# Packed dt weights, two-phase loading of SSD outputs and joined y products in a hybrid encoder layer

## The chip, the cores and the metric

The kernel runs on one core of a Trainium2 chip. The metric is the time of one execution in device microseconds (us). The programs have been run several times; the profile is one execution, taken by the hardware profiler. Its engines are PE (TensorE, matrix products, with PEld for its weight loads), DVE (VectorE), ACT (ScalarE), POOL (GpSimd) and SP (SyncE, which here issues every DMA).

## The reference, cut to what matters

One encoder layer over two requests of 256 tokens each (`x_prompt`, `x_sample`), model width 1024: a half-step FFN, one input projection `u @ w_in` that feeds three branches (neighbourhood attention, a bidirectional SSD, attention to a memory), a gated merge, and a second half-step FFN. The change touches the SSD branch:

```python
dt_f, dt_b = split_sizes(dt_raw, (SSD_HEADS, SSD_HEADS))          # 32 + 32 columns of u @ w_in
dt_f = softplus(dt_f + dt_bias_f);  a_f = -exp(a_log_f)           # the same for b
y_fwd = ssd_chunked(xs, dt_f, a_f, bm, cm)                        # 32 heads of 64, 8 groups, chunks of 128 tokens
y_bwd = flip(ssd_chunked(flip(xs), flip(dt_b), a_b, flip(bm), flip(cm)))
y_ssd = (y_fwd + y_bwd + ssd_d * xs) * silu(z)
o_ssd = grouped_rms_norm(y_ssd, ssd_norm, SSD_GROUPS)             # 8 groups of 256 channels
merged = g_na * (o_na @ w_br_na) + g_ssd * (o_ssd @ w_br_ssd) + g_mem * (o_mem @ w_br_mem)
```

## The kernel before

Both requests are worked on together: activations lie transposed, channels on the 128 partitions and 512 tokens (2 x 256) in a row. Weights are streamed once, in chunks of 128 x 1024 f32 (512 KB, tile `wr`, one DMA on SP's queue at L290) into a ring of 9 buffers (`RING`). `ahead()` splits each chunk into a high part `wh` (ACT, L322) and a low part `wl` (DVE, L236), and every product is made of three: high by high, high by low, low by high. A unit of the plan is 24 matmuls with 512 columns (L545 to L547 for `m` tiles, L1094 for the SSD branch's output projection), accumulated in one PSUM bank.

`PLAN` lists the units by hand. The side work of a stage (attention, SSD, norms) is a set of generators in a queue (`later`); `step()` moves the active ones on by one `yield` for each unit. The Tile scheduler then sets the order of each engine's instructions from that program order. Each engine and each DMA queue works through its own list in order.

The places that the change touches:

- `warm()` (L423 to L430). 16 matmuls on a zeroed tile `af` stand ahead of the first real product. POOL writes the zeroes (L425), then ACT makes a copy within the same tile so as to load its function table, then come the matmuls `wm` (L429; the profile shows two records for each).
- `do_dt` (L1131) and `t_dt` (L1138 on). The 64 dt columns of `w_in` are a unit of 24 matmuls with 64 output rows. `t_dt` then works softplus out on 64 x 512 tiles, transposes dt and a * dt with 8 transposes (`dtT`, L1166 and L1167) and copies them to `tokd`, tokens on partitions. Bias and a_log come from two columns of `params`.
- `t_ssd` (L1235 on), one generator for each of 8 groups. A group has two channel tiles i = 0, 1 of 128 channels. After the products CB (L1255), ACT and DVE make the decay tiles `e` for 8 cases (i, request b, head half hp). For each i and b, a run of 4 matmuls `y` (L1305) multiplies them: two output halves of 64 rows (hp) by two chunks (st), 8 records in the profile. Both runs of an i write one bank `y`, at steps n = 3, 5, 7 and 9 of the generator. After n = 5 and n = 9 DVE scales and gates the result; `rows_to_cols` (`sum`, L506), `spread` (`dg`, L514) and `spread_mm` (`R`, L523) make the group norm. Groups 0 to 5 write their result to DRAM (`scr_o`), and their norm factors to `scr_n`.
- `t_os(g)` (L1340) brings the results back. For groups 0 to 5 it loads the norm factors (`rw`, L1343), then for each i the result `or` (L1349), scales it at once (`scale_o`, on DVE) and splits it into `osh` (ACT) and `osl` (DVE). Groups 0 to 3 are handled while the eight SSD gates run (the last stage of L545 to L547 units before L1094), groups 4 to 7 after that. ACT turns each gate's bank into `tg` (L251).

Of the kernel before, what the change touches and what calls it, by code (L numbers as in the profile page):

```python
# [16 lines left out]
KD = 8  # L17
# [153 lines left out]
PCOLS = {}  # L171
_n = 0
for _name, _w in (("ffn1", 8), ("mix", 8), ("mem", 8), ("ffn2", 8), ("cw", 160), ("cb", 32), ("qn", 1), ("kn", 1),
                  ("mqn", 2), ("mkn", 2), ("sn", 16), ("dd", 16), ("dtb", 1), ("al", 1)):
    PCOLS[_name] = _n
    _n += _w
NPAR = _n
# [7 lines left out]
class Layer:  # L185
# [126 lines left out]
    def ahead(self, ci):  # L312

        for i in range(self.n_split, min(ci + 3, len(ITEMS))):
            it = ITEMS[i]
            self.fetch(i + self.depth)
            self.sums(i + 1)
            n = it.nk * it.m
            t = self.live[it.src]
            hi = self.pw.tile([128, 1024], F32R, tag="hi", name=self.name("wh"))  # L320
# [56 lines left out]
    def setup(self):  # L377
        nc = self.nc
        self.consts = self.pc.tile([128, NCONST], F32, name="consts")
        self.params = self.pc.tile([128, NPAR], F32, name="params")  # L380
        dma = nc.sync.dma_start
        self.x, self.depth = [], 0
        self.xs_start("ffn1")
        self.warm()
        dma(out=self.params[:, :32], in_=self.a["params"][:, :32])
        for c in range(4):
            for k in (2 * c, 2 * c + 1):
                self.x.append(self.g(p="x"))
# [15 lines left out]
        self.namask = c(8)[:, :64].rearrange("p (n k) -> p n k", n=2)  # L404
        self.lots = self.pc.tile([128, 4, 64], F32, name="lots")
# [723 lines left out]


    def do_dt(self, key, cis):  # L1131
        ps = self.unit(cis, self.u, m=64)

        def evac():
            self.later("dt", self.t_dt(ps))
        return evac

    def t_dt(self, ps):  # L1138
        V, S, T = self.V, self.S, self.T
        r = slice(0, 64)  # L1140
        v, m, e, z, w = (self.g(p="dt") for _ in range(5))
        self.act(v[r], ps[r], AF.Identity, bias=self.par("dtb", 0, r))
        self.ts(m[r], v[r], 0.0, ALU.max)
        self.stt(e[r], v[r], -1.0, v[r], ALU.mult, ALU.min)
        self.act(e[r], e[r], AF.Exp)
        yield
        self.ts(w[r], e[r], 2.0, ALU.add)
        V.reciprocal(w[r], w[r])
        self.tt(z[r], e[r], w[r], ALU.mult)
        yield  # L1150
        self.tt(w[r], z[r], z[r], ALU.mult)
        self.ts(e[r], w[r], 1.0 / 15, ALU.mult)
        for k in (13, 11, 9, 7, 5, 3):
            self.stt(e[r], e[r], 1.0 / k, w[r], ALU.add, ALU.mult)
            if k == 9:
                yield
        self.stt(e[r], e[r], 1.0, z[r], ALU.add, ALU.mult)
        self.stt(v[r], e[r], 2.0, m[r], ALU.mult, ALU.add)
        ea = self.small(2, "ea")
        self.act(ea[r, 0:1], self.par("al", 0, r), AF.Exp)  # L1160
        self.ts(w[r], v[r], ea[r, 0:1], ALU.mult, -1.0, ALU.mult)
# [6 lines left out]
        tk = self.pc.tile([128, 4, 128], F32, name="tokd")  # L1168
        V.tensor_copy(tk.rearrange("p t c -> p (t c)"), ps)
        self.tok = tk  # L1170
        yield
        rs = self.g(p="rs").rearrange("p (b l) -> p b l", b=2)
        for b in range(2):
# [58 lines left out]
    def t_ssd(self, g):  # L1232
# [62 lines left out]
        for n in range(10):  # L1295
            if n < 6:
                rw[n + 2] = self.rows(g, *heads[n + 2])
            if n >= 3 and n % 2:
                i, b, _ = heads[n - 3]
                w = [ws.pop(n - 3), ws.pop(n - 2)]  # L1300
                if b == 0:
                    yb = self.bank("y")
                for st in range(2):
                    for hp in range(2):
                        T.matmul(yb[64 * hp:64 * hp + 64, b * 256:(b + 1) * 256],  # L1305
                                 xt[i][:, (2 * b + st) * 128 + 64 * hp:(2 * b + st) * 128 + 64 * hp + 64],
                                 w[hp][0][:, 2 * st:2 * st + 2, :], start=st == 0, stop=st == 1)
# [12 lines left out]
            yield  # L1320
# [17 lines left out]
        self.stt(v, v, self.half[:, 2 * g + i:2 * g + i + 1], r, ALU.mult, ALU.mult)  # L1338

    def t_os(self, g):  # L1340
        if g < KEEP:
            r, sn = self.g(p="rw"), self.scr_n
            self.nc.sync.dma_start(out=r, in_=bass.AP(sn.tensor, sn.offset + g * 512, [[0, 128], [1, 512]]))  # L1343
        for i in range(2):
            k = 2 * g + i
            t = self.oraw.pop(k, None)
            if t is None:
                t = self.g(p="or")
                self.nc.sync.dma_start(out=t, in_=self.scr_o[k])  # L1349
                self.scale_o(g, i, t, r)  # L1350
            self.os[k] = self.split_tile(t, "os")
        return
        yield


def layer_kernel(tc, aps):
# [7 lines left out]
def layout(inp):  # L1364
# [31 lines left out]
    put("dtb", np.concatenate([f("dt_bias_f")[0], f("dt_bias_b")[0]])[:, None])  # L1396
    put("al", np.concatenate([f("a_log_f")[0], f("a_log_b")[0]])[:, None])

    i = np.arange(128)
    c = np.zeros((128, NCONST), np.float32)  # L1400
# [2 lines left out]
    for k, t in enumerate(tri):  # L1403
# [17 lines left out]
    return {"w": w, "xT": chan("x_prompt", "x_sample"), "memT": chan("mem_prompt", "mem_sample"), "params": p,  # L1421
            "consts": c, "strip": np.ascontiguousarray(strip.reshape(8, 128, 512))}


# [19 lines left out]
```

## Time and profile before

| | |
|---|---|
| time, median of 3 runs | 1757.79 us (1756.99 to 1758.3) |
| the profiled execution | 1756.64 us |
| its span, first to last instruction | 1754.9 us |
| PE busy | 1737.2 us (99%) |
| DVE busy | 1234.6 us (70%) |
| ACT busy | 848.0 us (48%) |
| DMA | 209.69 MB, mean 119 GB/s |

Busy times say how much of the span an engine had an instruction in work. The list of waits says for each engine and line how long it stood idle before such an instruction and what released it, in total, how often, and the longest. The chain of waits is followed back from the last instruction: at each step to what released it. Starts in the chain are moved to the end of what went before, so they can differ by some tenths of a us from the timeline, whose matmul records overlap.

### The profile page before, as it was taken

How to read it: one execution, taken by the hardware profiler on the slowest of the kernel's cores; microseconds unless marked ns; L12 is line 12 of the kernel's file. 1: busy time of each engine (PE TensorE's matmuls, PEld its weight loads, DVE VectorE, ACT ScalarE, POOL GpSimd, SP SyncE). 2: the span in 40 equal slices, each digit the busy share in tenths (PEclk: the TensorE clock that was granted, in tenths of full speed). 3: DMA queues.
4: the chain of work that ended last, by engine and by line, in shares of the span. 5: the costliest groups of instructions: out<-in, count | busy, mean ns of one | idle time of the engine just before them, and what ended most of it. 6: DMA issues, size and time to landing. Idle time of an engine off the chain costs nothing.

```text
span 1754.9 us, 22611 instructions
## 1 busy us (share of the span) xinstructions
PE 1737.2 (99%) x8568; PEld 1419.9 (81%) x8568; DVE 1234.6 (70%) x2056; ACT 848.0 (48%) x1515; POOL 0.7 (0%) x5
## 2 busy tenths in 40 slices
PE   9999999999999999999999999999899999999999
PEld 7888888988788888788877777777688878888887
DVE  7676776876544467835778888888753697776775
ACT  6443443543224336533666766766532464444442
POOL 0000000000000000000000000000000000000000
PEclk9999999999999999999999999999999999999999
DMA  6144233442323232333344545446433234244331
GB/s 258 60 143 144 97 107 134 155 156 89 96 77 104 88 103 85 102 109 97 120 127 127 132 139 136 123 138 175 162 126 121 84 109 138 79 153 127 99 115 48
DMA packets 79708, 209.69 MB, mean 119 GB/s; under 512 B 11120, under 2 KB 19696, under 8 KB 79600
## 3 DMA queue, kind: packets, MB, share of 16 engines
q1 hardware_dynamic: 79600, 208.26, 37.6%
q8 instruction: 67, 1.10, 0.3%
q14 instruction: 41, 0.34, 0.1%
HBM read 198.64 MB, written 9.58 MB: 119 GB/s over the span
## 4 chain that ended last, share of the span: by engine, by line
PE 96%; DVE 2%; DMA 1%; ACT 1%; issue 0%; SPq 0%; DVEq 0%; ACTq 0%
PE ac L567 20%; PE m L545 10%; PE m L546 10%; PE m L547 10%; PE q L589 5%; PE q L591 5%; PE q L590 5%; PE m L1094 5%; PE d L546 5%; PE d L547 5%; PE d L545 5%; PE y L1305 2%; PE hT L692 1%; PE CB L1255 1%; PE q L609 1%; PE q L611 1%
## 5 line engine op out<-in xcount | busy, mean ns | idle before, releaser
L322 ACT CAST wh<-wr 128x1024 fp32r<-128x1024 f32 (+1 forms) x357 | 371.2, 1040 | 686.5 <-PE ac L567 167.1
L236 DVE TENSOR_TENSOR wl<-wr,wh 128x1024 fp32r<-128x1024 f32 (+1 forms) x357 | 431.5, 1209 | 264.4 <-ACT wh L322 259.4
L545 PE MATMUL m<-uh,wh 128*128 128x512 f32 (+1 forms) x584 | 234.9, 402 | 6.7 <-ACT tg L251 6.7
L567 PE MATMUL ac<-wh,sh 128*128 128x512 f32 (+1 forms) x616 | 229.4, 373 | 0.5 <-ACT wh L322 0.5
L546 PE MATMUL m<-ul,wh 128*128 128x512 f32 (+1 forms) x584 | 229.6, 393 | 0.0
L567 PE MATMUL ac<-wl,sh 128*128 128x512 f32 (+1 forms) x616 | 228.1, 370 | 0.7 <-DVE wl L236 0.7
L547 PE MATMUL m<-uh,wl 128*128 128x512 f32 (+1 forms) x584 | 228.5, 391 | 0.0
L567 PE MATMUL ac<-wh,sl 128*128 128x512 f32 (+1 forms) x616 | 228.0, 370 | 0.0
L545 PEld LDWEIGHTS m<-uh,wh 128*128 128x128 f32 (+1 forms) x584 | 109.6, 188 | 38.3 <-ACT tg L251 6.9
L546 PE MATMUL d<-hl,wh 128*128 128x512 f32 x352 | 137.2, 390 | 0.7 <-DVE hl L236 0.7
L545 PE MATMUL d<-hh,wh 128*128 128x512 f32 x352 | 137.4, 390 | 0.5 <-ACT hh L258 0.5
L547 PE MATMUL d<-hh,wl 128*128 128x512 f32 x352 | 137.0, 389 | 0.0
L567 PEld LDWEIGHTS ac<-wl,sh 128*128 128x128 f32 x616 | 116.1, 188 | 20.6 <-DVE wl L236 1.3
L567 PEld LDWEIGHTS ac<-wh,sh 128*128 128x128 f32 x616 | 116.0, 188 | 20.6 <-ACT wh L322 1.3
L567 PEld LDWEIGHTS ac<-wh,sl 128*128 128x128 f32 x616 | 116.0, 188 | 19.7
L547 PEld LDWEIGHTS m<-uh,wl 128*128 128x128 f32 (+1 forms) x584 | 109.6, 188 | 24.6 <-issue 0.4
L546 PEld LDWEIGHTS m<-ul,wh 128*128 128x128 f32 (+1 forms) x584 | 109.7, 188 | 23.6 <-issue 1.5
L247 DVE SCALAR_TENSOR_TENSOR x<-d,x 128x512 f32<-128x512 f32 x96 | 66.2, 690 | 76.5 <-PE d L547 76.0
L589 PE MATMUL q<-wh,uh 128*128 128x512 f32 x256 | 102.9, 402 | 0.0
L236 DVE TENSOR_TENSOR wr<-wr,wr 128x1024 f32<-128x1024 f32 x80 | 97.6, 1221 | 6.3 <-DMA wr<-in_w 5.3
L591 PE MATMUL q<-wl,uh 128*128 128x512 f32 x256 | 99.9, 390 | 0.0
L590 PE MATMUL q<-wh,ul 128*128 128x512 f32 x256 | 99.9, 390 | 0.0
(253 smaller groups left out, 2857.6 us busy)
## 6 DMA issues: line engine op xcount, KB each, us to landing
wr<-in_w SPq DMA_DIRECT2D x308, 512.0 KB
rw<-scr_r SPq DMA_DIRECT2D x64, 256.0 KB
nv<-scr_v SPq DMA_DIRECT2D x64, 64.0 KB
scr_o<-cv SPq DMA_DIRECT2D x12, 256.0 KB
or<-scr_o SPq DMA_DIRECT2D x12, 256.0 KB
wr<-in_w SPq DMA_DIRECT2D x9, 256.0 KB
x<-in_xT SPq DMA_DIRECT2D x8, 256.0 KB
mr<-in_memT SPq DMA_DIRECT2D x8, 256.0 KB
```

The lines of the kernel that those rows point to most:

```text
L236: self.V.tensor_tensor(out=out, in0=a, in1=b, op=op)
L247: self.V.scalar_tensor_tensor(out=out, in0=a, scalar=s, in1=b, op0=op0, op1=op1)
L322: self.S.copy(hi[:, :n], t[:, :n])
L545: self.T.matmul(ps[:m], wh[:, kk, :], xh, start=i == 0, stop=False)
L546: self.T.matmul(ps[:m], wh[:, kk, :], xl, start=False, stop=False)
L547: self.T.matmul(ps[:m], wl[:, kk, :], xh, start=False, stop=i == n - 1)
L567: go = lambda l, r, **f: self.T.matmul(ps, l, r, skip_group_check=True, **f)
L589: self.T.matmul(self.qb[t], xh, wh[:, kk, :], start=k == 0, stop=False)
L590: self.T.matmul(self.qb[t], xl, wh[:, kk, :], start=False, stop=False)
L591: self.T.matmul(self.qb[t], xh, wl[:, kk, :], start=False, stop=k == KD - 1)
L1094: go = lambda l, r, **f: self.T.matmul(ps, l, r, skip_group_check=True, **f)
L1305: T.matmul(yb[64 * hp:64 * hp + 64, b * 256:(b + 1) * 256], xt[i][:, (2 * b + st) * 128 + 64 * hp:(2 * b + st) * 128 + 64 * hp + 64], w[hp ...
```

## The change

There are four edits.

1. **dt.** High and low part of the 64 dt columns lie side by side in one tile of 128 columns. One matmul with the high part of `u` makes high by high and low by high in 128 output rows, a second with the low part of `u` adds to the first 64: 16 matmuls in place of 24. `t_dt` copies the bank, transposes first (4 transposes of 128 x 128) and works softplus out on 128 x 256 tiles; bias and a_log come as a row `dtrow`, broadcast by a new DMA.
2. **y.** The two runs of an i (one for each request) become one run of 8 matmuls, sixteen records, at n = 5 and n = 9.
3. **t_os.** Both `or` loads of a group are issued with the load of the norm factors; after two `yield`s come the scaling and the split.
4. **warm.** ACT's copy works on a small tile `wm` of its own.

```diff
@@ ahead
+            if it.m == 64:
+                both = self.pw.tile([128, 1024], F32R, tag="hi", name=self.name("wh"))
+                v = both.rearrange("p (k m) -> p k m", k=it.nk)
...
+                self.S.copy(v[:, :, :64], raw)
+                self.tt(v[:, :, 64:], raw, v[:, :, :64].bitcast(F32), ALU.subtract)
...
@@ constants
+        self.dtrow = self.pc.tile([128, 128], F32, name="dtrow")
+        rows = self.a["dtrow"]
+        dma(out=self.dtrow, in_=bass.AP(rows.tensor, rows.offset, [[0, 128], [1, 128]]))
@@ warm
-        self.act(z[:, :1], z[:, 1:2], AF.Copy)
+        y = self.small(2, "wm")
+        self.G.memset(y, 0.0)
+        self.act(y[:, :1], y[:, 1:], AF.Copy)
@@ do_dt
-        ps = self.unit(cis, self.u, m=64)
+        ps = self.bank()
...
+        for k in range(KD):
+            xh, xl = self.u[k]
+            self.T.matmul(ps, w[:, k, :], xh, start=k == 0, stop=False, skip_group_check=True)
+            self.T.matmul(ps[:64], w[:, k, :64], xl, start=False, stop=k == KD - 1, skip_group_check=True)
@@ t_dt
+        raw = self.g(p="dt")
+        S.copy(raw, ps)
+        yield
+        ps = self.bank("dtT")
+        for t in range(4):
+            c = slice(t * 128, (t + 1) * 128)
+            T.transpose(ps[:, c], raw[:, c], self.ident)
...
-        for t in range(4):
-            s = slice(t * 128, (t + 1) * 128)
-            T.transpose(ps[:, t * 128:t * 128 + 64], v[r, s], self.ident[r, 0:64])
-            T.transpose(ps[:, t * 128 + 64:(t + 1) * 128], w[r, s], self.ident[r, 0:64])
...
@@ t_ssd
-            if n >= 3 and n % 2:
-                i, b, _ = heads[n - 3]
-                w = [ws.pop(n - 3), ws.pop(n - 2)]
-                if b == 0:
-                    yb = self.bank("y")
-                for st in range(2):
-                    for hp in range(2):
...
+            if n in (5, 9):
+                i = heads[n - 3][0]
+                yb = self.bank("y")
+                for b in range(2):
+                    w = [ws.pop(n - 5 + 2 * b), ws.pop(n - 4 + 2 * b)]
+                    for st in range(2):
+                        for hp in range(2):
...
@@ t_os
+        ks = (2 * g, 2 * g + 1)
         if g < KEEP:
             r, sn = self.g(p="rw"), self.scr_n
             self.nc.sync.dma_start(out=r, in_=bass.AP(sn.tensor, sn.offset + g * 512, [[0, 128], [1, 512]]))
-        for i in range(2):
-            k = 2 * g + i
-            t = self.oraw.pop(k, None)
-            if t is None:
-                t = self.g(p="or")
-                self.nc.sync.dma_start(out=t, in_=self.scr_o[k])
-                self.scale_o(g, i, t, r)
-            self.os[k] = self.split_tile(t, "os")
-        return
-        yield
+            for k in ks:
+                self.oraw[k] = self.g(p="or")
+                self.nc.sync.dma_start(out=self.oraw[k], in_=self.scr_o[k])
+            yield
+            yield
+            for i in range(2):
+                self.scale_o(g, i, self.oraw[ks[i]], r)
+        for k in ks:
+            self.os[k] = self.split_tile(self.oraw.pop(k), "os")
```

On PE, in a middle group of the SSD (`y` is the bank, `e` the decay tiles, `xt` the transposed channels; `m` and `uh`, `ul`, `wh`, `wl` belong to the units between), the runs of one i stand like this before:

```order
L547 MATMUL m1728_9332<-uh654_3388,wl1709_9203 128x512
L1305 MATMUL y1735_9381<-e1705_9192,xt1683_9075 64x256
L1305 MATMUL y1735_9381<-e1714_9254,xt1683_9075 64x256
L1305 MATMUL y1735_9381<-e1705_9192,xt1683_9075 64x256
L1305 MATMUL y1735_9381<-e1714_9254,xt1683_9075 64x256
L545 MATMUL m1737_9398<-uh608_3206,wh1717_9264 128x512
...
L547 MATMUL m1745_9446<-onh1277_6592,wl1731_9336 128x512
L1305 MATMUL y1735_9381<-e1727_9325,xt1683_9075 64x256
L1305 MATMUL y1735_9381<-e1736_9391,xt1683_9075 64x256
L1305 MATMUL y1735_9381<-e1727_9325,xt1683_9075 64x256
L1305 MATMUL y1735_9381<-e1736_9391,xt1683_9075 64x256
L545 MATMUL m1754_9508<-uh608_3206,wh1739_9401 128x512
```

and in the changed kernel like this:

```order
L563 MATMUL m1744_9433<-onh1277_6584,wl1731_9328 128x512
L1330 MATMUL y1751_9475<-e1704_9179,xt1683_9067 64x256
L1330 MATMUL y1751_9475<-e1714_9246,xt1683_9067 64x256
L1330 MATMUL y1751_9475<-e1704_9179,xt1683_9067 64x256
L1330 MATMUL y1751_9475<-e1714_9246,xt1683_9067 64x256
L1330 MATMUL y1751_9475<-e1727_9317,xt1683_9067 64x256
L1330 MATMUL y1751_9475<-e1735_9378,xt1683_9067 64x256
L1330 MATMUL y1751_9475<-e1727_9317,xt1683_9067 64x256
L1330 MATMUL y1751_9475<-e1735_9378,xt1683_9067 64x256
L561 MATMUL m1754_9500<-uh609_3211,wh1738_9388 128x512
```

The first run has moved down by 48 unit matmuls and stands right ahead of the second.

On SP, in the stretch of the SSD gates (`wr` is a weight chunk, `or` an SSD result, `rw<-scr_n` the norm factors of a group), the last loads before the output projection stand like this before:

```order
L290 DMA wr2025_11036<-in_w 128x1024
L1349 DMA or1993_10874<-scr_o_204 128x512
L290 DMA wr2036_11101<-in_w 128x1024
L1349 DMA or1996_10881<-scr_o_204 128x512
L290 DMA wr2041_11134<-in_w 128x1024
L1349 DMA or2003_10912<-scr_o_204 128x512
L1343 DMA rw2054_11230<-scr_n_203 128x512
L1343 DMA rw2065_11277<-scr_n_203 128x512
L290 DMA wr2047_11169<-in_w 128x1024
L1349 DMA or2006_10919<-scr_o_204 128x512
```

and in the changed kernel like this:

```order
L1369 DMA rw1987_10849<-scr_n_208 128x512
L1372 DMA or1988_10851<-scr_o_209 128x512
L1372 DMA or1989_10853<-scr_o_209 128x512
L1254 DMA rw1990_10855<-scr_r_207 128x512
L1369 DMA rw1998_10892<-scr_n_208 128x512
L1372 DMA or1999_10894<-scr_o_209 128x512
L1372 DMA or2000_10896<-scr_o_209 128x512
L290 DMA wr2025_11028<-in_w 128x1024
L290 DMA wr2036_11093<-in_w 128x1024
L290 DMA wr2041_11126<-in_w 128x1024
L290 DMA wr2047_11161<-in_w 128x1024
```

In the first list the last four `or` of the gates alternate with weight chunks, and the last one, `or2006`, stands behind `wr2047`; in the second they stand ahead of `wr2025`. The new `dtrow` load stands behind the `consts` load at the start.

## Rows read from the trace of the kernel before

**Rows 1.** The page: busy time, share of the span and instructions of each engine.
```profile
PE 1737.2 (99%) x8568; PEld 1419.9 (81%) x8568; DVE 1234.6 (70%) x2056; ACT 848.0 (48%) x1515; POOL 0.7 (0%) x5
```
**Rows 2.** Waits of PE: us in total, times, longest.
```profile
PE m L545 <- ACT tg L251: 6.7, 1, 6.7
```
**Rows 3.** Chain of waits at the last SSD gate: start us, us, what.
```profile
1261.53 0.33 SPq L290
1261.92 3.83 DMA or<-scr_o
1265.77 0.76 DVE or L247
1266.56 0.62 ACT osh L258
...
1267.72 0.79 PE m L545
...
1274.82 0.23 PE m L547
```
**Rows 4.** Windows of that wait: length; PE, PEld, DVE, ACT, POOL busy; PEclk, DMA.
```profile
1261.00:1267.70 6.70, 0.00 (x0) 0.00 (x0) 4.33 (x7) 1.76 (x4) 0.00 (x0) 0.75 0.51 158
1267.70:1271.30 3.60, 3.58 (x9) 2.85 (x10) 0.20 (x1) 1.92 (x4) 0.00 (x0) 0.51 0.00 0
1271.30:1275.00 3.70, 3.70 (x18) 3.08 (x17) 0.00 (x0) 0.14 (x1) 0.00 (x0) 1.00 0.00 0
```
**Rows 5.** Waits of SP's queue.
```profile
SPq L290 <- DVE wl L236: 1265.8, 263, 17.5
```
**Rows 6.** Stretches of the SSD gates' end and of a middle SSD group.
```profile
1230.00:1256.00 26.00, 26.00 (x121) 17.79 (x119) 22.41 (x43) 16.78 (x36) 0.00 (x0) 1.00 0.52 170
945.00:997.00 52.00, 52.00 (x249) 40.74 (x248) 44.43 (x93) 35.08 (x74) 0.00 (x0) 1.00 0.50 131
```
**Rows 7.** Chain of waits: a y run, the first and the eleventh matmul behind.
```profile
868.59 1.01 PE y L1305 x8
869.60 0.43 PE m L545
...
872.13 0.23 PE m L546
```
**Rows 8.** Chain of waits: a run of y with 10 records.
```profile
1230.57 1.44 PE y L1305 x10
```
**Rows 9.** Chain of waits: CB alone, and CB right behind a y run.
```profile
845.09 1.73 PE CB L1255 x8
...
894.83 1.92 PE CB L1255 x8
```
**Rows 10.** Timeline of PE: first dt matmul, and the first one behind them.
```profile
455.53 0.40 PE L545 MATMUL m<-uh,wh 128*64 128x512 f32 x1
...
461.05 0.39 PE L589 MATMUL q<-wh,uh 128*128 128x512 f32 x1
```
**Rows 11.** Chain of waits: dt's transposes, the matmul behind, four transposes of 128 x 128.
```profile
493.85 0.20 PE dtT L1166
...
494.49 0.43 PE q L589
...
531.04 0.44 PE amT L868 x4
```
**Rows 12.** Timeline of DVE: the last step of softplus in `t_dt`.
```profile
478.40 0.48 DVE L243 TENSOR_SCALAR dt<-dt,ea 64x512 f32<-64x512 f32 x1
```
**Rows 13.** Timeline of the start: the zeroes on POOL, the warm-up on PE.
```profile
0.73 0.52 POOL L425 MEMSET af<- 128x512 f32 x1 [0.29 <-POOLq L1428]
...
2.28 10.11 PE L429 MATMUL wm<-af 128*128 128x256 f32 x32 [2.28 <-ACT af L251]
```
**Rows 14.** Stretches of the warm-up.
```profile
2.28:8.20 5.92, 5.92 (x14) 4.71 (x15) 2.33 (x5) 3.42 (x7) 0.00 (x0) 1.00 0.95 321
8.20:12.00 3.80, 3.80 (x18) 3.35 (x18) 3.44 (x7) 3.67 (x7) 0.00 (x0) 1.00 1.03 403
```

More of the change, by code (lines that the diff above doesn't have):

```diff
@@ L173 @@
 for _name, _w in (("ffn1", 8), ("mix", 8), ("mem", 8), ("ffn2", 8), ("cw", 160), ("cb", 32), ("qn", 1), ("kn", 1),
-                  ("mqn", 2), ("mkn", 2), ("sn", 16), ("dd", 16), ("dtb", 1), ("al", 1)):
+                  ("mqn", 2), ("mkn", 2), ("sn", 16), ("dd", 16)):
     PCOLS[_name] = _n
@@ L319, in ahead @@
             t = self.live[it.src]
+            if it.m == 64:
+                both = self.pw.tile([128, 1024], F32R, tag="hi", name=self.name("wh"))
+                v = both.rearrange("p (k m) -> p k m", k=it.nk)
+                raw = t[:, :n].rearrange("p (k m) -> p k m", k=it.nk)
+                self.S.copy(v[:, :, :64], raw)
+                self.tt(v[:, :, 64:], raw, v[:, :, :64].bitcast(F32), ALU.subtract)
+                self.drop(it.src)
+                self.split[i] = v
+                self.n_split = i + 1
+                continue
             hi = self.pw.tile([128, 1024], F32R, tag="hi", name=self.name("wh"))
@@ L1131, in do_dt @@
     def do_dt(self, key, cis):
-        ps = self.unit(cis, self.u, m=64)
+        ps = self.bank()
+        ci, = cis
+        self.ahead(ci)
+        w = self.split.pop(ci)
+        for k in range(KD):
+            xh, xl = self.u[k]
+            self.T.matmul(ps, w[:, k, :], xh, start=k == 0, stop=False, skip_group_check=True)
+            self.T.matmul(ps[:64], w[:, k, :64], xl, start=False, stop=k == KD - 1, skip_group_check=True)
         def evac():
@@ L1140, in t_dt @@
         r = slice(0, 64)
[L1141 to L1145, printed above, removed]
-        yield
[L1147 to L1161, printed above, removed]
+        four = lambda z: z.rearrange("p (t c) -> p t c", t=4)
+        raw = self.g(p="dt")
+        S.copy(raw, ps)
         yield
@@ L1164, in t_dt @@
         for t in range(4):
-            s = slice(t * 128, (t + 1) * 128)
-            T.transpose(ps[:, t * 128:t * 128 + 64], v[r, s], self.ident[r, 0:64])
-            T.transpose(ps[:, t * 128 + 64:(t + 1) * 128], w[r, s], self.ident[r, 0:64])
-        tk = self.pc.tile([128, 4, 128], F32, name="tokd")
-        V.tensor_copy(tk.rearrange("p t c -> p (t c)"), ps)
-        self.tok = tk
+            c = slice(t * 128, (t + 1) * 128)
+            T.transpose(ps[:, c], raw[:, c], self.ident)
+        v, m, e, z, w = (self.g(p="dt")[:, :256] for _ in range(5))
+        tk = self.tok
+        row = lambda i: self.dtrow[:, 64 * i:64 * i + 64].unsqueeze(1).to_broadcast([128, 4, 64])
+        self.tt(four(v), four(ps)[:, :, 0:64], row(0), ALU.add)
+        self.tt(four(v), four(ps)[:, :, 64:128], four(v), ALU.add)
+        self.ts(m, v, 0.0, ALU.max)
+        self.stt(e, v, -1.0, v, ALU.mult, ALU.min)
+        self.act(e, e, AF.Exp)
+        yield
+        self.ts(w, e, 2.0, ALU.add)
+        V.reciprocal(w, w)
+        self.tt(z, e, w, ALU.mult)
+        yield
+        self.tt(w, z, z, ALU.mult)
+        self.ts(e, w, 1.0 / 15, ALU.mult)
+        for k in (13, 11, 9, 7, 5, 3):
+            self.stt(e, e, 1.0 / k, w, ALU.add, ALU.mult)
+            if k == 9:
+                yield
+        self.stt(e, e, 1.0, z, ALU.add, ALU.mult)
+        self.stt(tk[:, :, 0:64], four(e), 2.0, four(m), ALU.mult, ALU.add)
+        self.act(self.dtrow[:, 64:], self.dtrow[:, 64:], AF.Exp)
+        self.stt(tk[:, :, 64:128], tk[:, :, 0:64], -1.0, row(1), ALU.mult, ALU.mult)
         yield
@@ L1297, in t_ssd @@
                 rw[n + 2] = self.rows(g, *heads[n + 2])
-            if n >= 3 and n % 2:
-                i, b, _ = heads[n - 3]
-                w = [ws.pop(n - 3), ws.pop(n - 2)]
-                if b == 0:
-                    yb = self.bank("y")
-                for st in range(2):
-                    for hp in range(2):
-                        T.matmul(yb[64 * hp:64 * hp + 64, b * 256:(b + 1) * 256],
-                                 xt[i][:, (2 * b + st) * 128 + 64 * hp:(2 * b + st) * 128 + 64 * hp + 64],
-                                 w[hp][0][:, 2 * st:2 * st + 2, :], start=st == 0, stop=st == 1)
+            if n in (5, 9):
[5 more added lines that the diff above has]
+                        for hp in range(2):
+                            T.matmul(yb[64 * hp:64 * hp + 64, b * 256:(b + 1) * 256],
+                                     xt[i][:, (2 * b + st) * 128 + 64 * hp:(2 * b + st) * 128 + 64 * hp + 64],
+                                     w[hp][0][:, 2 * st:2 * st + 2, :], start=st == 0, stop=st == 1)
             if 1 <= n < 9:
@@ L1395, in layout @@
     put("dd", cols(np.repeat(f("ssd_d")[0], 64)))
-    put("dtb", np.concatenate([f("dt_bias_f")[0], f("dt_bias_b")[0]])[:, None])
-    put("al", np.concatenate([f("a_log_f")[0], f("a_log_b")[0]])[:, None])
+    dtrow = np.concatenate([f(n)[0] for n in ("dt_bias_f", "dt_bias_b", "a_log_f", "a_log_b")])
     i = np.arange(128)
@@ L1420, in layout @@
     strip = strip.reshape(8, 2, 128, 256).transpose(0, 2, 1, 3)
-    return {"w": w, "xT": chan("x_prompt", "x_sample"), "memT": chan("mem_prompt", "mem_sample"), "params": p,
+    return {"w": w, "xT": chan("x_prompt", "x_sample"), "memT": chan("mem_prompt", "mem_sample"), "params": p, "dtrow": dtrow,
             "consts": c, "strip": np.ascontiguousarray(strip.reshape(8, 128, 512))}
```

4 lines of the change are left out of this document (3 added, 1 removed).

## Prediction

> **What bounds the kernel now.** The busy times come first [rows 1]: PE works 1737.2 of 1754.9 us, DVE 70% and ACT 48% of it. The reader should see that only two things can shorten the run: less PE work, or less of the idle time of PE, some 17 us in all. The list of PE's waits is the second view. Its longest entry by far is one wait of 6.7 us at L545 for ACT's `tg` [rows 2]; nothing else there concerns the edits but the start of the warm-up. The chain of waits at that place is the third view [rows 3]: a weight fetch on SP, issued at 1261.53, then the last `or` load of the gates, 3.83 us until it has landed, its scaling on DVE, `osh` on ACT, and then only `tg`, which empties the bank that the last gate needs. The gate's 24 matmuls run from 1267.72 to 1275.05. In the windows of that stretch [rows 4] PE does nothing from 1261.0 to 1267.7, then 9 matmuls in 3.6 us at a granted clock of 0.51 (the lower level, 1.2 GHz), then 18 in 3.7 us at 1.00 (2.4 GHz). So the wait costs twice: the idle time, and a slow start after it.
>
> **Part 1, t_os.** At the unit pace of 0.23 us (24 matmuls in 5.52 us, [rows 10]) the last gate takes 5.5 us; it took 7.3 [rows 3]. Wait and slow start are 6.7 + 1.8 = 8.5 us. The edit issues all `or` loads of the gates ahead of `wr2025` in SP's queue; the last one then no longer stands behind `wr2047`, which was held until its chunk's buffer came free. Four weight fetches, one for each unit of 5.5 us and so some 20 us, lie between the two places. A load needs some 4 us to land [rows 3], so the data wait is gone. `tg` then stands behind an `osh` that doesn't wait. I take the whole 8.5 us. What is late next is DVE: from 1230 to 1256 it was busy 22.4 of 26.0 us [rows 6], and two scalings and two splits, some 0.75 us each [rows 3], that it did in the idle stretch (4.3 us of work there, [rows 4]) have to fit in ahead, 3.0 us into 3.6. That is just enough; I take 0 and keep 2 us as the upper end.
>
> What the `or` loads are moved past: row loads for the decay tiles and weight fetches on SP. Four issues in a row at some 0.4 us delay those behind by under 2 us. SP itself waits 1265.8 us in all, 263 times, for DVE to have done with a chunk [rows 5], that is, for a free buffer: the ring is full whenever it fetches, and 8 chunks at 5.5 us stand ahead. A delay of 2 us is hidden by 44; without that cover it would cost 2 us.
>
> **Part 2, y.** A run of 4 matmuls (8 records) takes 1.01 us, and the first unit matmul behind it 0.43 in place of 0.23 [rows 7]. From its start to the eleventh matmul behind are 3.54 us; less ten at 0.23 the run costs 1.24. A run of 5 matmuls takes 1.44 [rows 8], 0.43 more than one of 4: the two output halves go together, and a pair takes 0.43. A run of 8 then takes 1.01 + 2 x 0.43 = 1.87, and costs 1.24 + 0.86 = 2.10 with the same edges; two runs of 4 cost 2.48. One join saves 0.38. There are 14 outside the last group: 5.3 us. In 7 of them CB stood right behind a run and took 1.92, against 1.73 alone [rows 9]; counting by these, 1.01 + 1.92 + 1.24 become 1.73 + 2.10, and 0.34 is saved in place of 0.38, so 5.0 for the fourteen. The last group's runs are cut up, since its `e` tiles come late: 5, 3, 1, 3, 1, 3 matmuls before, 5, 3, 4, 1, 3 after, by the order. That is one run and one pair less, 0.38 + 0.43 = 0.8. The reading of 0.23 for the pace, rounded up, takes some 0.03 off each of the runs, so I take 6.0. The lower end is that a join saves only the one slow matmul, 0.20, 15 x 0.20 = 3.0; the upper end 6.6.
>
> Does the joined run wait? It stands where the second run of the pair stood, and needs nothing later than that one did. In a middle group PE is never idle and DVE busy 44.4 of 52.0 us [rows 6], so that `e` is ahead. Taken at 0.
>
> **Part 3, dt.** 24 matmuls with 64 output rows took 5.52 us [rows 10], 0.23 each, no less than those with 128. Eight fewer save 1.8. The eight small transposes take 0.64 until the next unit matmul, and that one 0.43 in place of 0.23; four of 128 x 128 take 0.44 [rows 11]. Saved 0.2 to 0.4, taken at 0.3. Part 3 gives 2.1. What hides the rest: from the end of the dt unit (461.05) to the last step of softplus (478.88) were 17.8 us [rows 10, 12], with, by the order, 144 unit matmuls between unit and transposes. Now 72 stand ahead of the transposes, 16.5 us for one copy of the bank, and 96 behind, 22.1 us for a chain that works on half as many elements per partition. Even at the old 17.8 us it fits. Uncovered it would cost the difference, 0 here; I keep 1 us. The `dtrow` load and its Exp stand at the start, 450 us before they are needed: 0.
>
> **Part 4, warm-up.** The zeroes are written by 0.73 + 0.52 = 1.25 us; the first warm-up matmul starts at 2.28, held by ACT's copy [rows 13]. It can start 1.0 us earlier. No gap stands between the last warm-up matmul and the first real one, so that all of it reaches the end if the pace pattern moves along: up to 8.20 us there were 14 records in 5.92 us, then 18 in 3.80 [rows 14], the slow stretch as at the lower level (the granted clock reads 1.00 in both windows and doesn't show it). I take 1.0. If the pace rises at the same moment as before, at 8.2 us, the extra 1.03 us holds 2.4 slow records, which would have taken 0.5 later: a gain of 0.5. The rows can't tell the two apart, since there is one start in them. The Trainium skill, page "TensorE: Matmul & The Clock Gate", section "What's actually happening", says that the window of the clock's gate runs freely and doesn't begin anew when a kernel starts. That speaks for the second, and no run here shows it; by it the sum is 0.5 us smaller.
>
> **Sum.** 8.5 + 6.0 + 2.1 + 1.0 = 17.6 us. The profiled execution took 1756.64 (1.7 around its span of 1754.9), so 1739.0; the median of the runs is 1.15 above it, so 1757.79 - 17.6 = **1740.2 us**. What a measurement can tell from no change is 0.2%, 3.5 us.
>
> **Rivals.**
> - *The clock keeps its moment.* The page's reading of the warm-up as above: 1740.7 us. For it: nothing in the trace ties the rise to the first matmul. Against: nothing either.
> - *DVE is the next to be late.* The scalings and splits, now ahead of the last gate, fill DVE (22.4 + 3.0 of 26.0), the low parts of the weights come late, and the last gates wait. If half of the idle time comes back with its slow start, that is 4.2 us: 1744.4. For it: [rows 6]. Against: DVE keeps some slack, and the shorter y runs hardly change its work.
> - *A joined run streams no better.* A join saves only the slow matmul behind: 3.0 in place of 6.0, 1743.2. Against it: the 0.43 for a further pair [rows 8].
> - *The gate is held all the same.* `tg` or the bank waits for something else than the `or` load, and the 8.5 us stay: 1748.7. Against: in the chain everything behind the load follows at once [rows 3].
> - *Slower: the `e` tiles are held too long.* A joined run frees the first request's tiles 48 matmuls, 11 us, later. If ACT and DVE then can't begin the next tiles and DVE's free 7.6 us in a group [rows 6] are used up, each of 14 runs waits 11 - 7.6 = 3.4 us: 47.6 - 17.6 = 30 us slower, 1788. It makes the kernel slower than the 0.2% from 1.5 us of wait per run, (17.6 + 3.5) / 14. Against: the waiting must come in every group, and PE now waits in none.
>
> **How the numbers follow.** Chances: the forecast 0.55, the clock's moment 0.15, DVE late 0.15, a join without gain in streaming 0.08, the gate held 0.05, slower 0.02. Forecast and first rival lie between 1737 and 1742, from the upper ends of the terms and the spread of the runs. The next two reach to 1745, with up to 2 us of new waits 1746.5. The range is 1736.5 to 1746.5; some 0.15 is left out. Faster by over 0.2% holds in all cases but the last, and in the last between no wait and 1.5 us a run it would be the same: faster 0.97, same 0.01, slower 0.02.
>
> **What would show it.** In the profile after: PE's wait at L545 for `tg` is gone, and no stretch near the last gate has a granted clock below 1; `y` comes in runs of 16 records of some 1.87 us in the chain; 16 dt matmuls in some 3.7 us; the first warm-up record near 1.25 us and the first real matmul near 11.0 (11.5 by the rival). Wrong would be a new wait on `wl` or `e` in PE's list of over 2 us, a wait of `wh` for its weight chunk between 1230 and 1290, or the old wait at another gate.

## The result, and the profile after

The changed kernel takes 1736.04 us (1735.5 to 1737.25, 4 runs) against 1757.39 (1756.61 to 1758.3): 21.4 us less, a ratio of 0.9879 with the interval 0.9862 to 0.9896. The forecast was 1740.2 us, 17.6 less than the median of that time; the measured time lies 0.46 us below the low end of the range. The direction held, and so did the mechanisms of three parts; that of the start did not, and the sum was too small. The miss of the range is small beside the noise: the kernel before, run again beside each set of experiments, had medians of 1757.21, 1756.98 and 1756.76 us, so differences of half a us between sets say nothing.

The page of the changed kernel, for [rows 1], and the beginning of its chain by engine:

```profile
PE 1724.5 (99%) x8556; PEld 1419.7 (82%) x8556; DVE 1225.5 (71%) x2057; ACT 846.8 (49%) x1515; POOL 0.8 (0%) x6
PE 97%; DVE 2%; ACT 0%; issue 0%; DMA 0%; POOL 0%; DVEq 0%; ACTq 0%; POOLq 0%
```

PE is busy for 12.7 us less, and the span is shorter by 21.2 (1733.7 against 1754.9); the other 8.5 us are idle time that went. PE's waits, in total, times, longest, for [rows 2]:

```profile
PE wm L445 <- POOL wm L441: 1.3, 1, 1.3
PE d L562 <- DVE hl L236: 0.7, 2, 0.4
PE qT L967 <- DVE nt L247: 0.7, 1, 0.7
```

The 6.7 us at `tg` are gone. The stretch from 1215 to 1255, in which the gates and the last group's norm now fall, in the columns of [rows 4], and the chain there (start, us, what), for [rows 3]:

```profile
1215.00:1255.00 40.00, 40.00 (x194) 30.34 (x193) 34.80 (x80) 24.42 (x49) 0.00 (x0) 1.00 0.52 167
```
```profile
1247.93 0.79 PE sum L522 x8
...
1254.09 7.93 PE m L1110 x35
```

PE is busy for all of the 40 us at a granted clock of 1.00. DVE has 34.8 of 40 us: close, as feared, but no wait of PE over 0.2 us comes from it.

To see where the time went, I numbered the unit matmuls with 128 output rows (512 columns) in both traces and compared their starts. The changed kernel is ahead by 2.2 us at the first one, 2.4 at 59 us, 4.6 behind dt and its transposes and up to 840 us, 10.8 when the fourteenth joined run is done, and 21.1 behind the last gate and to the end. By parts: start 2.4, dt 2.2, y in the groups 6.2, and 10.3 in the last stretch, of which the wait and its surroundings are 9.5 and the last runs of y 0.8.

For y, the chain with a joined run and the distance of two runs of `xT`, one in each group (first fence: after; second: before):

```profile
874.87 1.88 PE y L1330 x16
876.75 0.43 PE m L561
...
879.24 0.23 PE m L562
...
933.74 0.87 PE xT L1269 x8
...
985.06 0.87 PE xT L1269 x8
```
```profile
939.67 0.87 PE xT L1244 x8
...
991.87 0.87 PE xT L1244 x8
```

A run of sixteen records takes 1.88 us, as worked out (1.87); the line at 879.24 is the eleventh matmul behind it. A group takes 51.32 us in place of 52.20, so a join saves 0.44.

For dt, the first of the 16 matmuls and the first one behind them, for [rows 10] (timeline), and the transposes, for [rows 11] (chain):

```profile
453.09 0.39 PE L1155 MATMUL m<-uh,wh 128*128 128x512 f32 x1
...
456.79 0.39 PE L605 MATMUL q<-wh,uh 128*128 128x512 f32 x1
```
```profile
473.29 0.44 PE dtT L1172 x4
473.73 0.24 PE q L605
```

16 matmuls take 3.70 us, and the matmul behind four full transposes is not slowed: 0.24 in place of 0.43.

For the start, [rows 13] and [rows 14] have this as their answer (timeline with the first real matmul, then two windows):

```profile
1.31 8.84 PE L445 MATMUL wm<-af 128*128 128x256 f32 x32 [1.31 <-POOL wm L441]
...
9.80 0.58 PE L625 MATMUL q<-wh,sh 128*128 128x512 f32 x1
```
```profile
1.31:4.80 3.49, 3.49 (x8) 2.84 (x9) 0.00 (x0) 0.97 (x3) 0.00 (x0) 1.00 0.61 161
4.80:9.80 5.00, 5.00 (x25) 4.40 (x24) 3.33 (x7) 4.36 (x10) 0.00 (x0) 1.00 1.01 383
```

The first warm-up record starts 0.97 us earlier, but the first real matmul 2.24 us. The slow stretch was 8 records long and not 14. Neither the forecast nor its rival has that.

### The profile page after: what moved, and what is told of

Its sections match the earlier page's. It is cut to its first block, busy times and chain, and to the rows that moved or that the text cites. A ratio compares the mean times of both kernels' runs of the same rounds, so it can differ in the third digit from the quotient of the medians.

```text
span 1733.7 us, 22579 instructions
## 1 busy us (share of the span) xinstructions
PE 1724.5 (99%) x8556; PEld 1419.7 (82%) x8556; DVE 1225.5 (71%) x2057; ACT 846.8 (49%) x1515; POOL 0.8 (0%) x6
## 4 chain that ended last, share of the span: by engine, by line
PE 97%; DVE 2%; ACT 0%; issue 0%; DMA 0%; POOL 0%; DVEq 0%; ACTq 0%; POOLq 0%
PE ac L583 21%; PE m L561 10%; PE m L563 10%; PE m L562 10%; PE q L605 5%; PE q L607 5%; PE q L606 5%; PE m L1110 5%; PE d L562 5%; PE d L563 5%; PE d L561 5%; PE y L1330 2%; PE hT L708 1%; PE am L865 1%; PE amo L893 1%; PE CB L1280 1%
## 5 line engine op out<-in xcount | busy, mean ns | idle before, releaser
L561 PE MATMUL m<-uh,wh 128*128 128x512 f32 x576 | 229.7, 399 | 0.0
L563 PE MATMUL m<-uh,wl 128*128 128x512 f32 x576 | 225.0, 391 | 0.0
L562 PE MATMUL m<-ul,wh 128*128 128x512 f32 x576 | 224.8, 390 | 0.0
L561 PEld LDWEIGHTS m<-uh,wh 128*128 128x128 f32 x576 | 108.2, 188 | 27.8 <-ACT ct L251 5.0
L563 PEld LDWEIGHTS m<-uh,wl 128*128 128x128 f32 x576 | 108.1, 188 | 23.5 <-issue 0.8
L562 PEld LDWEIGHTS m<-ul,wh 128*128 128x128 f32 x576 | 108.3, 188 | 21.8 <-issue 0.4
```

The lines of the kernel that those rows point to most:

```text
L561: self.T.matmul(ps[:m], wh[:, kk, :], xh, start=i == 0, stop=False)
L562: self.T.matmul(ps[:m], wh[:, kk, :], xl, start=False, stop=False)
L563: self.T.matmul(ps[:m], wl[:, kk, :], xh, start=False, stop=i == n - 1)
```

## The experiments

There are twelve runs: ten kernels, and both kernels once more. The theory after the result: each part is worth what its place in the trace shows, and the start is worth 1.0 in the mean, since the moment at which the pace rises is not tied to the first matmul. The expectations reckon with 9.3 us for the last gate, 7.0 for y and up to 2.4 for dt, where the starts above give 9.5, 7.0 and 2.2. Rivals: the start is worth 2.2; or the parts help each other.

**1. The warm-up alone.**

```diff
@@ warm, in the kernel before
-        self.act(z[:, :1], z[:, 1:2], AF.Copy)
+        y = self.small(2, "wm")
+        self.G.memset(y, 0.0)
+        self.act(y[:, :1], y[:, 1:], AF.Copy)
```

> The kernel before with the edit of the warm-up alone. Both theories: the first warm-up record starts near 1.3 us in place of 2.28. Theory 'the start decides': the pace of the warm-up rises 3.5 us after its first record, as in the changed kernel (4.81 - 1.31), and the first real matmul starts near 9.8 us, 2.2 us earlier than in the kernel before. Theory 'the moment is not tied to the start': the time from the first record to the rise is any between 3.4 and 6.8 us, another one than 3.5, and the first real matmul starts between 9.8 and 11.5 us. In time: 1756.2 to 1755.2, ratio 0.9987 to 0.9994.

Measured: 1756.9 us, ratio 0.9999 (0.9989 to 1.0008). The pace rose 5.7 us after the first record, not 3.5, and the first real matmul started at 10.91. So the moment of the rise is not set by the first record. At the end the trace is 1.1 us later than that of before, all the same: it lost 0.4 us by 41 us, 1.0 at `ns` (0.9 of it a wait, below) and 1.0 at the last gate, where the slow stretch was longer. A gain of 1.0 us is within the interval, so is none.

**2. The loads alone** (the `t_os` hunk of the change, in the kernel before).

```diff
@@ t_os
...
+            for k in ks:
+                self.oraw[k] = self.g(p="or")
+                self.nc.sync.dma_start(out=self.oraw[k], in_=self.scr_o[k])
+            yield
+            yield
...
```

> The kernel before with the two-phase loading alone. Theory 'the last load stood behind a weight fetch': the wait of 6.7 us at the last SSD gate and the slow matmuls behind it are gone, and nothing else moves: 8.4 to 9.3 us less, 1748.1 to 1749.0, ratio 0.9947 to 0.9952. Rival 'the gate is late by the load on VectorE too': a wait of 1 us or more for wl, e or tg stands in the gates' list, 1750 or more. The warm-up starts at 2.28 as before: if its start decides, the pace rises 6.1 us after the first record as in the profile of before (8.35 - 2.28); if not, at another distance.

Measured: 1747.67 us, ratio 0.9943 (0.9927 to 0.996), 9.5 us less. The wait is gone; the longest ones left on PE, but for the start's, are these (in total, times, longest):

```profile
PE q L609 <- ACT up L629: 0.9, 1, 0.9
...
PE ns L981 <- ACT npT L1009: 0.7, 1, 0.7
```

The pace rose 3.15 us after the same first start of 2.28 that had 6.07 in the profile of before. The first real matmul came 1.35 us earlier, and by 41 us 1.2 of that was lost again, 0.9 of it in the wait for `up` at 36 us.

**3. The joined y runs alone** (the `t_ssd` hunk, in the kernel before).

```diff
@@ t_ssd
-            if n >= 3 and n % 2:
+            if n in (5, 9):
...
+                for b in range(2):
...
```

> The kernel before with the joined y runs alone; the loads of the SSD results keep their code, but the scheduler now puts the last one ahead of the weight fetch behind which it stood. Theory 'the weight fetch in front of the load is the cause': the wait of 6.7 us at the last gate goes without the two-phase loading, and the time falls by 7.0 for y and up to 9.3 for the wait, to 1741 to 1745 (ratio 0.991 to 0.993). Rival 'the load and its use stand too close whatever is between them': some wait of 2 to 7 us stays, and the time is 1745 to 1750.5. In a middle group the distance of two xT runs falls from 52.20 to 51.3 us, 0.44 for each joined run.

Measured: 1748.42 us, ratio 0.9951 (0.9936 to 0.9966). The time fits the rival, and so does the wait:

```profile
PE m L545 <- ACT tg L251: 4.3, 1, 4.3
```

In this kernel the last `or` load was issued at 1249.84, ahead of the last weight fetch (1255.17), and its scaling began at 1256.98, 7.1 us later. So the weight fetch in front of it is not the whole cause; experiment 9 shows the rest. The gain of 8.8 us is more than y: part of the gate's wait is in it.

**4. dt alone** (the hunks of `ahead`, the constants, `do_dt` and `t_dt`, in the kernel before).

```diff
@@ do_dt
-        ps = self.unit(cis, self.u, m=64)
...
+            self.T.matmul(ps, w[:, k, :], xh, start=k == 0, stop=False, skip_group_check=True)
+            self.T.matmul(ps[:64], w[:, k, :64], xl, start=False, stop=k == KD - 1, skip_group_check=True)
```

> The kernel before with the packed dt weights alone. 16 matmuls in 3.68 us in place of 24 in 5.52, four transposes in place of eight: 2.1 to 2.4 us less, 1755.1, ratio 0.9987. The wait at the last gate stays at 6.7 us. Rival 'the longer chain from dt to its rows is uncovered': a wait of PE on row or dtT, and less than 1.5 us gained. The warm-up starts at 2.28: if its start decides, its pace rises 6.1 us after the first record; if not, at another distance.

Measured: 1754.6 us, ratio 0.9984 (0.9975 to 0.9994), 2.6 us less. PE waits for neither `dtT` nor `row`; the gate's wait stays at 6.4. The pace rose after 5.2 us. One thing came with this edit that nobody asked for: the 0.5 us of waits at `hT` for `sg`, near 58 us, which every trace with the old dt has (before, experiments 1, 2, 3 and 11), are in none of the nine with the new one (four of these have 0.2 to 0.8 us at `hT` for another tile).

**5. All but y** (the changed kernel with the `t_ssd` of before).

```diff
@@ t_ssd, in the changed kernel
-            if n in (5, 9):
...
+            if n >= 3 and n % 2:
...
```

> The changed kernel with the y runs of before (four matmuls for each request). Theory 'a join is worth 0.44 us in the trace': the distance of two xT runs is 52.2 us again in place of 51.3, the wait at the last gate stays away, and the time is 7.0 us above the changed kernel's 1736.0: 1743.0. Rival 'the edits help each other': single edits gave 0.3 (warm-up), 9.5 (loads) and 2.6 (dt) of the 21.4, which leaves 8.9 for y: 1745, with waits of PE of 1 to 2 us that the changed kernel does not have.

Measured: 1744.73 us, 8.7 above the changed kernel (ratio to before 0.9931, 0.9916 to 0.9945). In the trace, two `xT` runs are 52.20 us apart again (936.68 and 988.88), and y alone makes 6.9 us of the trace's 9.3 between this kernel and the changed one. The rest lies elsewhere: the start (0.6), the first 60 us (0.4), `ns` (0.6), the norm's `sum` (0.4) and the beginning of the second FFN (0.4). The theory holds for y. The time is the rival's, and so are small waits of PE that the changed kernel doesn't have: 0.6 at `ns`, 0.4 more at `sum` and 0.3 at `hT`. Whether they belong to the missing edit or to this one execution, one trace can't say.

**6. All but the warm-up** (the changed kernel with the `warm` of before).

```diff
@@ warm, in the changed kernel
-        y = self.small(2, "wm")
-        self.G.memset(y, 0.0)
-        self.act(y[:, :1], y[:, 1:], AF.Copy)
+        self.act(z[:, :1], z[:, 1:2], AF.Copy)
```

> The changed kernel with the warm-up of before, first record at 2.28. Theory 'the rise is not tied to the start': the pace rises somewhere between 3.1 and 6.8 us after it, and over many runs the edit is worth its 1.0 us or less: 1736.0 to 1737.0. Rival 'the edit is worth the 2.2 us that the two profiles show at the first real matmul': 1738.2.

Measured: 1737.05 us, ratio to before 0.9887 (0.987 to 0.9903), 1.0 above the changed kernel. That is nearer to 1.0 than to 2.2, but the interval holds both, and nothing as well.

**7. Loads early, no yields.**

```diff
@@ t_os, in the changed kernel
-            yield
-            yield
+            if False:
+                yield
```

> The changed kernel without the two yields in t_os: the loads of a group still stand together ahead of the weight fetches, but scaling and split follow at once in program order. Theory 'the place of the loads in SP's queue decides': no wait at the last gate, 1736 as the changed kernel. Rival 'the yields decide, since scaling and split otherwise stand ahead of the decay tiles on VectorE and wait there for the load': a wait of 1 to 7 us in the gates, 1737 to 1745.

Measured: 1738.47 us, ratio to before 0.9895 (0.9881 to 0.991). The time lies in the rival's range, but its wait is not there: the early loads keep the gate free without the yields. From the first real matmul, 1.33 us late here by the pace, the trace loses another 1.2 by the end, all in the last group: its y falls into 3, 1, 3, 1, 3 matmuls behind the first five in place of 3, 4, 1, 3, and `R` comes late by 0.25 us. The windows of its warm-up show the slow stretch with the new start at its longest:

```profile
1.31:7.40 6.09, 6.09 (x14) 4.87 (x15) 1.09 (x3) 2.54 (x6) 0.00 (x0) 1.00 0.72 212
7.40:11.10 3.70, 3.70 (x19) 3.23 (x17) 2.44 (x5) 3.01 (x7) 0.00 (x0) 1.00 1.03 413
```

**8. A shorter warm-up.**

```diff
-RING, DEPTH, WARM = 9, 8, 16
+RING, DEPTH, WARM = 9, 8, 12
```

> The changed kernel with 12 warm-up matmuls (24 records) in place of 16. The first chunk's low part is ready at 9.4 us (8.16 + 1.23). Theory 'the warm-up only has to last until the first chunk is split': the first real matmul starts at 8.5 to 9.5 us and up to 1.2 us are gained, 1734.8 to 1736. Rival 'what starts earlier waits later for the side work': a wait of PE for up or for a chunk between 12 and 60 us takes it back, 1736.

Measured: 1736.5 us, ratio to before 0.9886 (0.9871 to 0.9901), no difference from the changed kernel. The pace rose after 5.7 us; the 24 records were through some 0.3 us before the first chunk was split:

```profile
9.82 0.50 PE L625 MATMUL q<-wh,sh 128*128 128x512 f32 x1 [0.28 <-ACT wh L332]
```

So up to about 9.8 us the data set the start, and the quickest warm-up of 16, at 9.80, loses nothing. The others with the new start end at 10.4 to 11.1; what a shorter one is worth against those, these runs don't resolve.

**9. All but the loads** (the changed kernel with the `t_os` of before).

```diff
@@ t_os, in the changed kernel
...
+        for i in range(2):
...
+            t = self.oraw.pop(k, None)
+            if t is None:
+                t = self.g(p="or")
+                self.nc.sync.dma_start(out=t, in_=self.scr_o[k])
+                self.scale_o(g, i, t, r)
...
```

> The changed kernel with the loading of before, one load, scaling and split after the other. In e3_y_only the last load stood ahead of the last weight fetch but behind others, and a wait of 4.3 us was left. Theory 'place in the queue, in steps': the wait at the last gate is some 4 us again and the matmuls behind it start slowly, 5.5 to 7 us in all: 1741.5 to 1743. Rival 'the two edits are independent': 9.3 us as in the change from before, 1745.

Measured: 1745.53 us, 9.5 above the changed kernel (ratio to before 0.9937, 0.992 to 0.9954): the rival's time, with the theory's wait. The wait at the last gate is 4.3 us. The chain ahead of it:

```profile
1246.23 3.60 DMA rw<-scr_n
...
1250.04 0.75 DVE or L247
1250.78 0.39 DVE dg L530 x2
1251.17 1.14 DVE wl L236
1252.31 0.60 DVE osl L236
1252.91 1.32 DVE cv L247 x2
1254.23 0.67 DVE or L247
...
1254.92 0.62 ACT osh L258
1255.54 0.51 ACT tg L251
```

The last load, and where DVE's stretch of work begins (timeline):

```profile
1247.08 0.42 SPq L1374 DMA_DIRECT2D or<-scr_o  x1
```
```profile
1247.46 0.16 DVE L272 TENSOR_SCALAR v<-sum 128x4 f32<-128x4 f32 x1 [0.43 <-PE sum L522]
```

The last load was issued 7.1 us before its scaling; if it took the 3.6 us of the load in the chain, it had landed over 3 us before (an estimate). The chain has a load of norm factors, `rw`, at its head, but between 1247.46 and the last scaling DVE has no gap over 0.04 us: its own list is the bound. The norm's small steps, an earlier scaling, `dg`, a weight's low part, a split and the gating all stand ahead of the last scaling, and only then come `osh` and `tg`. In between `R` waits for `dg`: 1.0 us in all on PE's list, against 0.5 before. And the slow start behind the shorter wait is longer (windows in the columns of [rows 4]):

```profile
1251.70:1256.00 4.30, 0.05 (x1) 0.00 (x0) 3.62 (x6) 1.08 (x3) 0.00 (x0) 0.90 0.55 187
1256.00:1262.10 6.10, 6.01 (x14) 4.72 (x15) 0.27 (x1) 1.99 (x5) 0.00 (x0) 0.51 0.00 0
```

By the starts, 14 matmuls took 6.02 us, 2.8 more than at the full pace, against 1.7 more in the profile of before. So 4.3 us of wait cost 7.1 us with the slow start, where 6.7 had cost 8.4.

**10. Yields, but late loads.**

```diff
@@ t_os, in the changed kernel
-            for k in ks:
-                self.oraw[k] = self.g(p="or")
-                self.nc.sync.dma_start(out=self.oraw[k], in_=self.scr_o[k])
             yield
             yield
...
+        for i in range(2):
...
+                t = self.g(p="or")
+                self.nc.sync.dma_start(out=t, in_=self.scr_o[k])
+                self.scale_o(g, i, t, r)
...
```

> The changed kernel with the two yields kept but the result loads issued after them, each right ahead of its scaling. Theory 'the place of the loads in the queue decides': with the loads among or behind the weight fetches the wait of 4 us or more at a gate is back, 1741 to 1747. Rival 'the yields alone do it': 1736.

Measured: 1743.02 us, ratio to before 0.9922 (0.9908 to 0.9937). A wait of 4.0 us is back, now at the first unit of the output projection (DVE's timeline, chain, windows):

```profile
1256.14 1.23 DVE L236 TENSOR_TENSOR wl<-wr,wh 128x1024 fp32r<-128x1024 f32 x1 [1.67 <-ACT wh L332]
```
```profile
1257.37 0.67 DVE or L247
...
1258.06 0.62 ACT osh L258
1258.68 0.51 ACT tg L251
...
1259.23 4.84 PE m L1110 x13
```
```profile
1255.70:1259.70 4.00, 0.47 (x2) 0.43 (x3) 2.58 (x3) 2.04 (x5) 0.00 (x0) 1.00 0.30 65
1259.70:1263.70 4.00, 4.00 (x13) 3.11 (x12) 1.12 (x2) 2.04 (x4) 0.00 (x0) 0.57 0.51 201
```

So the yields alone don't do it; the place of the loads does. Here too the chain runs through DVE's list: the scaling stands behind the low part of a weight, which waited 1.67 us for `wh`, and the load itself had been issued at 1252.18. The granted clock here is 1.00 throughout the wait and 0.57 in the four us behind it, when PE was at work again.

**11 and 12. Both kernels again,** unchanged.

> The kernel before once more, for its trace. Theory 'the rise is not tied to the start': the pace of the warm-up rises at another distance from the first record than 6.1 us (so far 3.1 to 6.1), and the waits of 0.6 to 0.9 us at ns near 670 us, which four of the other traces show, may be there. Rival: 6.1 us again, and no such wait.

> The changed kernel once more, for its trace. Theory: the rise comes at another distance than 3.5 us from the first record, and the first real matmul by so much later. Rival: 3.5 us again. The last gate has no wait in either case, and the distance of two xT runs is 51.3 us.

Measured: 1757.16 and 1736.46 us in one execution each. In the kernel before, the pace rose 4.0 us after the first record, where it had been 6.1; in the changed one after 4.8, where it had been 3.5. The first real matmuls are then at 11.08 and 10.49 us, 0.6 apart and not 2.2. The waits of the kernel before, this time:

```profile
PE m L545 <- ACT tg L251: 6.8, 1, 6.8
...
PE ns L981 <- ACT npT L1009: 1.0, 1, 1.0
...
PE hT L692 <- DVE sg L247: 0.5, 2, 0.3
```

The wait at `ns` (neighbourhood attention, near 670 us) was not in the profile that the prediction was made from. The traces with the old dt have 0, 0.9, 0.7, 0.9 and 1.0 us of it, those with the new one 0 in seven of nine, and 0.6 and 0.4. In each trace with 0.6 us or more DVE's waits for the load of the attention's bias strip are longer, 5.0 to 6.8 us in all against 3.5 to 4.3. That it comes less often with the new dt is seen, not explained.

## Why the prediction was wrong, point by point

The mechanisms of the gate, y and dt were right. Two steps failed: the size of the y term (a join saves 0.44 us, not 0.38), and 'nothing else there concerns the edits', by which the waits at `R` and `hT`, 0.5 us each, stood in the sum with nothing. The mechanism of the start was wrong too, at a price that no run resolves.

**The last gate, forecast 8.5, measured 9.1 to 9.5** (9.5 in the pair of profiles and by the medians of experiments 2 and 9, 9.1 in the trace of experiment 2). The mechanism was right: in [rows 3] the late load is the head of the chain, and with early loads the wait and the slow start are gone (experiments 2 and 7), while without them, or with yields alone, a wait of 4 us and more is back (9 and 10). Two things were missed. The norm's `R` had a wait of its own in the same stretch (timeline; first fence: before; second: after):

```profile
1259.01 0.39 PE L547 MATMUL m<-uh,wl 128*128 128x512 f32 x1
1259.87 1.13 PE L523 MATMUL R<-dg,consts 128*128 128x128 f32 x8 [0.48 <-DVE dg L514]
1267.72 0.79 PE L545 MATMUL m<-uh,wh 128*128 128x512 f32 x1 [6.72 <-ACT tg L251]
```
```profile
1251.89 0.39 PE L562 MATMUL m<-ul,wh 128*128 128x512 f32 x1
1252.12 1.05 PE L539 MATMUL R<-dg,consts 128*128 128x128 f32 x8
1252.93 0.48 PE L563 MATMUL m<-uh,wl 128*128 128x512 f32 x1
```

From the matmul ahead of `R` to the one behind it were 8.71 us, now 1.04: 7.7 less, not 6.7. Of the difference 0.5 is `R`'s wait, and 0.5 the ends of two records (modelled in the profile) that the next ones no longer overlapped. The slow start makes 1.7 more. PE's list of waits had a line for `R`, 0.5 us, and the prediction said that nothing else there concerned the edits. And the story was too simple: with the load moved ahead of the last weight fetch alone, DVE's list holds the gate by 4.3 us. The rival 'DVE is the next to be late' named the right engine, and it came true in a kernel that moves the loads half way, not in this one.

**y, forecast 6.0, measured 6.9 to 7.0.** The step that failed is 'one join saves 0.38': it saved 0.44. The run of 8 was right, 1.88 us for 1.87. The pace was not: that of ordinary units is 0.2267 (7.93 us for 35 in the chain above), not the 0.23 that was read off the dt matmuls [rows 10], which are slower than the others (3.70 us for 16 here again). With 0.2267 a run of 4 costs 3.54 - 2.27 = 1.27, and a joined one 874.87 to 879.24, 4.37 - 2.27 = 2.10; two runs less a joined one are 0.44. The forecast's 2.10 for the joined run is the same number by luck: its own steps with the right pace give 1.27 + 0.86 = 2.13. So the pace makes one half of the 0.06, and the other half is that the ten matmuls behind a joined run take 0.03 to 0.04 us less than those behind a run of 4. The joins with CB behind them, priced at 0.34, saved 0.42, by the starts. The correction for the rounded pace added 0.2 us to the sum of 5.8 where 1.1 to 1.2 were needed. No join waited, and the slow rival fell.

**dt, forecast 2.1, measured 2.2 in the trace,** 1.8 for the matmuls and 0.4 for the transposes; the term was right. What the sum put at nothing is the DVE order near 58 us without the 0.5 us of waits at `hT`, also a line of that list of waits. In the pair of profiles these 0.5 stand in the 2.4 of the start.

**The start, forecast 1.0, 2.2 in the pair of profiles, 0.3 and 1.0 in the single edits.** The forecast let the pace move along with the first record, the rival held its moment fixed. Both are wrong: in thirteen warm-ups of 16 matmuls and one of 12, the rise came 3.2 to 6.1 us after the first record, with the old start after 6.1, 3.2, 3.6, 5.2, 4.4 and 4.0 us, with the new one after 3.5, 5.7, 4.8, 6.1, 4.4, 6.1, 4.8 and 5.7. 3.2 is less than the 3.4 that I had expected as the least, and no run shows the 6.8 that I gave as the most. So 1.3 us between the two profiles are chance. In the mean the first real matmul came at 11.25 us in the six traces with the old start and at 10.59 in the seven with the new one and 16 matmuls: 0.7 us of the edit's 1.0, part of which later waits (`up` in experiments 2 and 4) take back. No time of a kernel shows a gain clear of the noise. The page "TensorE: Matmul & The Clock Gate" of the Trainium skill, section "What's actually happening", says that the window of the clock's gate runs freely, so that the moment depends on where in it the first matmul lands. That the moment varies, the traces show too; the half a us either way that the page gives it, they don't: here the spread is 3 us, and that decides. The conclusion I drew from it, that the moment stays at 8.2 us, was mine and wrong.

**The sum.** By the traces the parts are 9.5 + 7.0 + 2.2 + 0.7 and the 0.5 at `hT`: 19.9 of the 21.4 us between the medians. The wait at `ns` makes some 0.6 in the mean of the traces. And the slow start behind the gate's wait was a short one in the profile of before, 1.7 us lost; in the other three traces with that wait (experiments 1, 4 and 11) it lost 2.5, 2.7 and 2.4, which makes 0.6 more in the mean. What is left, 0.3 us, is less than the spread of the runs. That the parts add up so well is in part luck: the interval of the ratio is 18.3 to 24.3 us. The range failed because its low end was built from the upper ends of the four terms and the spread alone; the small things left out, waits that go along with a change of order, lay on the same side.

## What to carry to other kernels

Price an edge between two kinds of matmul with the pace of the same matmuls in a long stretch (0.2267), not with a rounded one of others subtracted ten times, and check it by the distance of two like places (52.20 against 51.32 us a group). Go through the whole list of waits: each line in a stretch that a change reorders is a term, even at 0.5 us. A wait behind a late load is to be followed through the list of the engine that uses the load: moving the load by one place freed the DMA and left 4.3 of 6.7 us standing in DVE's list, and the kernel 9.5 us slower. And where a start or a restart of PE is costed from one profile, the slow stretch is a draw, 1.5 to 2.8 us lost here behind a wait, and a difference of two profiles holds two draws.

## What the runs showed of the hardware

The length of the slow stretch behind a wait does not follow the wait: 6.4 to 6.9 us of idle PE were followed by 3.5 to 5.7 us at the lower level in four traces (before 3.5, experiments 11, 1 and 4 4.8, 5.2 and 5.7), 4.3 us by 3.1 us in experiment 3 and by 6.0 in 9, and in experiment 10 the granted clock was 1.00 in the 4.0 us of the wait and 0.57 in the four behind it. In the warm-up the granted clock in the rows reads 1.00 in both stretches (experiment 7), though the records start 0.43 us apart in the first and 0.22 in the second; the column doesn't show the slow stretch. And 64 output rows are no cheaper here than 128 with 512 columns: 24 matmuls with 64 rows took 5.52 us, and 16 of which half have 128 rows 3.70, 0.23 each.
